# Branch A of an encoder layer: one round of transposes per step in place of two, with the scores behind it

## The chip, the core and the metric

The kernel runs on one core of a Trainium2 chip. The core has five engines with a queue each, and each queue runs its instructions in the order in which they were written. PE (TensorE) multiplies matrices and transposes tiles by multiplying with an identity; its results go to the eight banks of PSUM. DVE (VectorE) and ACT (ScalarE) read PSUM and SBUF, POOL (GpSimd) works on SBUF and issues some of the transfers, and SP (SyncE) issues the rest. An engine that needs another's result waits for a semaphore, and all that stands behind the waiting instruction waits too. The metric is the device time of one execution in microseconds, the median of several.

## The reference

An encoder layer is applied to a sample of 1024 positions and a prompt of 256, model width 1024. The part that matters here is branch A, an attention with 8 query heads of width 64 that share 2 key and value heads, a window of 128 positions to each side, a bias table and a sink per head:

```python
s = jnp.einsum('bnqgrd,bnkgd->bngrqk', qb, kb).astype(jnp.float32) * (dh ** -0.5)
...
logits = jnp.where(valid[None, :, None, None], s + bias, NEG_INF)
m = jnp.max(logits, axis=-1)
...
p = jnp.exp(logits - m[..., None])
denom = jnp.sum(p, axis=-1)
...
o = jnp.einsum('bngrqk,bnkgd->bnqgrd', p.astype(vb.dtype), vb).astype(jnp.float32)
```

A second branch (B, dilated windows) runs earlier in the kernel. Both are merged by gates, go through an output product and a squared-ReLU MLP, and a final norm. Everything is float32; the large products are split into high and low parts and multiplied in three passes.

## The kernel before, in words

Branch A covers 40 tiles: 4 units (two heads each) by 10 tiles of 128 queries (8 of the sample, 2 of the prompt). A tile sees W = 256 or 384 keys: three blocks of 128 inside the sample, two at its ends and for the prompt's tiles. The order of instructions is written out by hand. The main loop takes tiles two at a time, j = 0, 2, ... 40; I call one pass of it a step. In it stand:

- `scores(u, t)`: four products on PE into two banks of the tag `sc` (one per head), a DVE instruction per head that adds the bias, writes the logits `s` to SBUF and keeps the maximum, and a small DVE instruction, a SCALAR_TENSOR_TENSOR on line 1137, that makes the negated maximum `nm_a` of both heads.
- `exponential(u, t, h)`: ACT turns `s` into exp(s - maximum) in place, once per head.
- `transposes(u, t)`: PE transposes the 4 or 6 blocks of `s` into banks of the tag `pt`, four blocks to a bank; ACT moves the first bank to SBUF, DVE the second (lines 272 and 274).
- `values_of(u, t)`: PE multiplies values by the transposed weights of two tiles into the one bank of tag `pv`; DVE copies it out and POOL sends it to DRAM.
- `next(fill)`: one portion of an unrelated product, the plain gate logits (line 192): four matmuls of 512 columns or eight of 256. It fills PE's queue between the pieces of attention. At the end of a 512- or 256-column block ACT copies the bank out (`gs`), and after each 256-column block the next weights are split into `whi` (ACT) and `wlo` (DVE, line 235).
- `next(merges)`: one piece of the merging of branch B, work of POOL, DVE, ACT and the DMA queues (lines 1248 to 1272 on DVE, 1310 and 1313 on POOL).

PSUM has three banks of tag `mm` for the fill, two `sc`, two `pt`, one `pv`. Scores of step j are turned round by `transposes` in step j + 2 and used by `values_of` in step j + 4. Before the change a step in the middle is, on PE: scores, portion, values, portion, transposes of one tile, scores, portion, transposes of the other tile.

Of the kernel before, what the change touches and what calls it, by code (L numbers as in the profile page):

```python
# [15 lines left out]
P = 128  # L16
# [34 lines left out]
HALVES = (slice(0, HD), slice(HD, P))  # L51
# [46 lines left out]
def encoder_kernel(  # L98
# [5 lines left out]
    nc = tc.nc  # L104
# [31 lines left out]
    def bank(tag, name=None):  # L136
        return psum.tile([P, 512], F32, name=name or tag, tag=tag, bufs={"mm": 3, "sc": 2, "pt": 2, "pv": 1}[tag])
# [108 lines left out]
    ident = const.tile([P, P], F32, name="ident")  # L246
# [22 lines left out]
    def moved(eng, out, in_):  # L269

        if eng is nc.scalar:
            nc.scalar.activation(out, in_, AF.Copy)  # L272
        else:
            nc.vector.tensor_copy(out, in_)
# [48 lines left out]
    def steps_of(gen, n):  # L323
        for _ in range(n):
            next(gen, None)
# [152 lines left out]
    def attention_b(make):  # L478
# [21 lines left out]
        def load(j):  # L500

            if j >= n:
                return
            g, i, t, (pieces, W, _) = order[j]
            qk = held[j] = [make("qk", (P, 3 * P), n=4), None]
            for src, at, m, o in ((scr_qb[g][i], [x[2] for x in pieces], pieces[0][1], 0),
                                  (scr_kb[g][i], [x[3] for x in pieces], W, P)):
                if len(pieces) == 1:
# [8 lines left out]
        def load_v(j):  # L517
            if not 0 <= j < n:
                return
            g, i, t, (pieces, W, _) = order[j]  # L520
            v = held[j][1] = make("v", (P, 2, P), n=6)
            for a, (_, _, _, ka) in enumerate(pieces):
                for k in range(W // P):
                    nc.sync.dma_start(v[:, a + k, :], values_rows(g, i, ka // P + k))

        def scores(j):
# [4 lines left out]
            for k in (j, j + 1):  # L531
                g, i, t, (pieces, W, c0) = order[k]
                qk = held[k][0]
                for h in range(2):
                    rows = HALVES[h]
                    for a, (p0, nq, _, _) in enumerate(pieces):
                        nc.tensor.matmul(at(k, h)[p0 : p0 + nq, :], qk[rows, p0 : p0 + nq],  # L537
                                         qk[rows, P + P * a : P + P * a + W], start=True, stop=True,
                                         skip_group_check=True)
# [129 lines left out]
    with ExitStack() as pre:  # L669
# [195 lines left out]
        for t in range(2, NT):  # L865
# [13 lines left out]
            ps = bank("mm", "v")  # L879
# [20 lines left out]
        for t in (4, 5, 6, 7, 8, 9, 0, 1, 2, 3):  # L900
            ps = bank("mm", "v")
# [6 lines left out]
    if True:  # L908
# [177 lines left out]
        b, p = iter(()), parts0  # L1086
        att_b = iter(())
        for first, last, name in ((0, MIXED, "pairs"), (MIXED, len(PAIRS), "mixed")):
            with tc.tile_pool(name=name, bufs=1) as now[0]:
                if first:  # L1090
                    att_b = attention_b(stage)
                for j in range(first, last):
# [4 lines left out]
                    b, p = pair(b, p, PAIRS[j], PAIRS[j + 1] if j + 1 < len(PAIRS) else None, hooks, tick, first)  # L1097
# [10 lines left out]
    if True:  # L1108
# [4 lines left out]
        def a3(name, shape=(P, 2, 3 * P), n=3, dt=F32):  # L1113
            return att.tile(list(shape), dt, name=name, tag=name, bufs=n)

        tiles = []
# [4 lines left out]
        live, units = {}, {}  # L1121
# [19 lines left out]
        def exponential(u, t, h):  # L1141
            W, s = tiles[t][1], live[u, t]
            nc.scalar.activation(s[:, h, :W], s[:, h, :W], AF.Exp, bias=nm_a[:, 2 * u + h : 2 * u + h + 1, t],
                                 accum_out=l_a[:, 2 * u + h : 2 * u + h + 1, t])

        def transposes(u, t):

            W = tiles[t][1]
            s = live[u, t]
            pt = a3("pt", (P, 6, P), 2)  # L1150
            jobs = [(b, h) for b in range(W // P) for h in range(2)]
            for i, eng in ((0, nc.scalar), (4, nc.vector))[: 1 + (len(jobs) > 4)]:
                ps, e = bank("pt"), min(len(jobs), i + 4)
                for k, (b, h) in enumerate(jobs[i:e]):
                    nc.tensor.transpose(ps[:, P * k : P * k + P], s[:, h, P * b : P * b + P], ident)  # L1155
                moved(eng, pt[:, i:e, :], ps[:, : P * (e - i)].rearrange("p (i q) -> p i q", q=P))
            live[u, t] = pt

        def values_of(u, t):

            pv = bank("pv")
            for i in range(2):
                lo, W, _ = tiles[t + i]
                pt = live.pop((u, t + i))
                v, rest = units[u][0]["v"]
                for b in range(W // P):
                    k = lo + b
                    src = v[:, k, HALVES[u // 2]] if k < 8 else rest[:, k - 8, HALVES[u // 2]]
                    for h in range(2):
                        nc.tensor.matmul(pv[HALVES[h], P * i : P * i + P], src, pt[:, 2 * b + h, :],  # L1170
                                         start=b == 0, stop=b == W // P - 1, skip_group_check=True)
            o = a3("o", (P, 2, P), 2)
            nc.vector.tensor_copy(o, pv[:, : 2 * P].rearrange("p (i q) -> p i q", i=2))
            nc.gpsimd.dma_start(scr_o[t // 2][:, u], o)
# [156 lines left out]
    if True:  # L1331
# [53 lines left out]
        order = [(u, t) for u in range(4) for t in range(NT)]  # L1385
        n = len(order)
        fill = logits()
        merges = merge()
        next(merges)
        steps_of(fill, 2)  # L1390
        for j in range(0, n + 2, 2):
            if j < n:
                scores(*order[j])
                next(fill)
                for h in range(2):
                    exponential(*order[j], h)
            if j > 2:
                values_of(*order[j - 4])
                if j < n:
                    next(merges, None)  # L1400
            next(fill)
            if j:
                transposes(*order[j - 2])
            if j == n:
                next(fill)
            if j < n:
                scores(*order[j + 1])
                next(fill)
            if j:
                transposes(*order[j - 1])  # L1410
                if j > 2:
                    next(merges, None)
            if j < n:
                for h in range(2):
                    exponential(*order[j + 1], h)
            if j == n - 4:
                high_b(0)
                low_b(0)
            if j < n and order[j][1] == 0 and order[j][0] < 3:
                u = order[j][0] + 1  # L1420
                units[u] = load_unit(u), load_bias(u, lambda name, shape: a3(name, shape, 2))
            if j in (n - 6, n - 4):
                fetch()
            if j == n - 2:
                load_o(0)
                load_o(1)
# [9 lines left out]
        jobs = [(x, b, c) for b in range(3) for x in "ba" for c in range(KC if x == "b" else 4)]  # L1436
# [41 lines left out]
        for i, (x, b, c) in enumerate(jobs):  # L1478
            t0, n = BLOCKS[b]
# [13 lines left out]
            per, src = (4, (ob_hi, ob_lo)) if x == "b" else (2, (o_hi, o_lo))  # L1493
            cols = slice(P * (c % per), P * (c % per) + P)
            ps = bank("mm")
# [79 lines left out]
    with ExitStack() as pre:  # L1575
# [20 lines left out]
        for hh in range(2):  # L1596
# [17 lines left out]
            for t in range(NT):  # L1614
                m = parts.pop(t)
                ps = bank("mm")
# [43 lines left out]
    class Down:  # L1660
# [4 lines left out]
        def make(self, name, shape=(P, 2, 512), dt=F32):  # L1665
            return self.late.tile(list(shape), dt, name=name, tag="l4", bufs=8)
# [196 lines left out]
    with ExitStack() as pre:  # L1863
# [106 lines left out]
        b = b0, p0  # L1970
        down = Down()
        last = FF // P // 2 - 1
        for j in range(last + 1):
            b = up(j, *b, entering() if not j else down.begin() if j == last else iter(()))
# [26 lines left out]
```

## Time and profile before

| | us |
|---|---|
| median of 3 runs (1690.64 to 1692.21) | 1692.16 |
| the profiled execution | 1693.05 |
| its span, first to last instruction | 1691.3 |
| branch A's loop, from 543.7 to 679.7 of the span | 136.0 |

On the whole span PE is busy 1670.7 us (99%), DVE 950.1, ACT 721.3 and POOL 514.9. A busy share close to one means that little idle time is left to remove; it does not say that the matrix engine works at its peak. The timeline's rows give start, duration, engine, line, operation, output and inputs, shape and count, and in brackets the idle time before the row and what ended it. Matmuls overlap, so what one costs is read from the distance between starts: 0.23 us for 512 columns, 0.12 for 256, about 0.11 for a transposed block, while their durations are 0.39, 0.28 and 0.27.

### The profile page before, as it was taken

Reading aid. Unit: us, or ns where it says so; the run is one execution under the profiler, and the core shown is the slowest. Engines: PE = TensorE matmul, PEld = TensorE weight load, DVE = VectorE, ACT = ScalarE, POOL = GpSimd, SP = SyncE. Lnnn points to the kernel's source line nnn. Section 1 sums busy time; section 2 is a strip of 40 time slices with the busy share of each in tenths; the row PEclk is TensorE's granted clock in tenths of the full one; section 3 lists DMA queues with packets and bytes.
Section 4 is the critical chain, followed back from the end, with each engine's and each line's share of the span. In section 5 each row is a group of like instructions: output and inputs, shape, how many; then the busy total and the mean of one; then the engine's idle time right before and its main releaser. Section 6 shows DMA issues by size and latency. Waiting matters only on the chain.

```text
span 1691.3 us, 24932 instructions
## 1 busy us (share of the span) xinstructions
PE 1670.7 (99%) x9268; PEld 1414.9 (84%) x9268; DVE 950.1 (56%) x1548; ACT 721.3 (43%) x1489; POOL 514.9 (30%) x404
## 2 busy tenths in 40 slices
PE   8999999999999999999999999999999999999998
PEld 7898888887788888888888888888887888888886
DVE  6733233455563565667378445455457767667575
ACT  6332323356562656654176333333334333333345
POOL 1312212212112472200100556455556322314150
PEclk9999999999999999999999999999999999999999
DMA  7416562567666893845121443343346744633333
GB/s 246 151 57 125 134 136 75 162 192 200 182 196 193 219 245 100 289 136 189 41 85 58 159 159 118 121 159 130 116 152 250 280 152 157 209 106 116 119 119 124
DMA packets 224408, 260.35 MB, mean 154 GB/s; under 512 B 29568, under 2 KB 154288, under 8 KB 224288
## 3 DMA queue, kind: packets, MB, share of 16 engines
q1 hardware_dynamic: 214976, 235.60, 43.9%
q0 software_dynamic: 7936, 20.54, 5.6%
q10 hardware_dynamic: 1376, 2.62, 0.4%
q8 instruction: 73, 1.20, 0.3%
q14 instruction: 47, 0.39, 0.1%
HBM read 173.03 MB, written 90.92 MB: 156 GB/s over the span
## 4 chain that ended last, share of the span: by engine, by line
PE 90%; DVE 4%; ACT 2%; DMA 2%; issue 1%; POOL 1%; SPq 0%; DVEq 0%; ACTq 0%; POOLq 0%
PE dn L347 20%; PE x L347 18%; PE mm L192 14%; PE z L347 9%; PE v L794 6%; PE mm L347 5%; PE y L347 5%; PE sc L347 2%; PE pv L347 2%; PE sc L537 1%; PE pv L1170 1%; PE pv L582 1%; PE pt L569 1%; PE pt L1155 1%; PE sc L1131 1%
## 5 line engine op out<-in xcount | busy, mean ns | idle before, releaser
L347 PE MATMUL dn<-dhi,ulo 128*128 128x512 f32 x448 | 175.7, 392 | 4.3 <-DVE ulo L186 4.3
L347 PE MATMUL dn<-dlo,uhi 128*128 128x512 f32 x448 | 175.2, 391 | 0.0
L347 PE MATMUL dn<-dhi,uhi 128*128 128x512 f32 x448 | 175.1, 391 | 0.0
L347 PE MATMUL x<-chi,wlo 128*128 128x512 f32 x424 | 167.3, 395 | 1.7 <-DVE wlo L314 1.6
L347 PE MATMUL x<-clo,whi 128*128 128x512 f32 x424 | 165.7, 391 | 0.1
L347 PE MATMUL x<-chi,whi 128*128 128x512 f32 x424 | 165.1, 389 | 0.0
L314 DVE TENSOR_TENSOR wlo<-ta,whi 128x1024 fp32r<-128x1024 f32 x30 | 55.7, 1857 | 179.1 <-ACT whi L312 179.1
L314 DVE TENSOR_TENSOR wlo<-raw,whi 128x1024 fp32r<-128x1024 f32 x60 | 92.5, 1541 | 96.7 <-ACT whi L312 96.7
L389 POOL TENSOR_TENSOR tb<-raw 128x512 f32<-128x512 f32 x25 | 32.7, 1308 | 364.4 <-DMA raw<-in_w_in_dram 147.8
L347 PEld LDWEIGHTS dn<-dhi,ulo 128*128 128x128 f32 x448 | 84.6, 189 | 23.2 <-DVE ulo L186 5.7
L186 DVE TENSOR_TENSOR ulo<-uraw,uhi 128x1024 fp32r<-128x1024 f32 x56 | 94.3, 1702 | 12.4 <-ACT uhi L185 12.4
L347 PEld LDWEIGHTS dn<-dhi,uhi 128*128 128x128 f32 x448 | 84.7, 189 | 17.8
L347 PEld LDWEIGHTS dn<-dlo,uhi 128*128 128x128 f32 x448 | 84.7, 189 | 17.4
L347 PEld LDWEIGHTS x<-chi,wlo 128*128 128x128 f32 x424 | 79.8, 188 | 18.1 <-DVE wlo L314 1.3
L347 PEld LDWEIGHTS x<-chi,whi 128*128 128x128 f32 x424 | 79.6, 188 | 17.0
L1699 POOL TENSOR_TENSOR t<-raw,t 128x1024 f32<-128x1024 f32 x16 | 47.7, 3001 | 147.0 <-DMA raw<-in_w_down_dram 147.0
L347 PEld LDWEIGHTS x<-clo,whi 128*128 128x128 f32 x424 | 79.8, 188 | 14.8 <-DVE clo L314 0.4
L1853 DVE TENSOR_TENSOR v<-v,dn 128x512 f32<-128x512 f32 x90 | 59.6, 681 | 40.4 <-PE dn L347 37.9
L1946 POOL TENSOR_TENSOR u<-u,u 128x640 f32<-128x640 f32 x16 | 26.1, 1630 | 160.0 <-ACT u L1871 160.0
L347 PE MATMUL dn<-dhi,up 128*128 128x512 f32 x224 | 73.5, 389 | 0.0
L347 PE MATMUL z<-chi,wlo 128*128 128x512 f32 x184 | 72.0, 391 | 0.0
L272 ACT ACTIVATE pt<-pt 128x512 f32<-128x512 f32 (+1 forms) x70 | 37.9, 543 | 79.5 <-PE pt L1155 45.0
(325 smaller groups left out, 4660.9 us busy)
## 6 DMA issues: line engine op xcount, KB each, us to landing
scr_u<-u SPq DMA_DIRECT2D x112, 320.0 KB, 2.6
uraw<-scr_u SPq DMA_DIRECT2D x56, 512.0 KB, 4.5
raw<-in_w_in_dram SPq DMA_DIRECT2D x33, 512.0 KB, 5.4
raw<-in_w_up_dram SPq DMA_DIRECT2D x32, 512.0 KB, 5.2
raw<-in_w_down_dram SPq DMA_DIRECT2D x28, 512.0 KB, 6.6
sg<-scr_g SPq DMA_DIRECT2D x32, 256.0 KB, 6.4
uraw<-scr_u SPq DMA_DIRECT2D x28, 256.0 KB, 4.7
v<-scr_v SPq DMA_DIRECT2D x96, 64.0 KB, 2.7
```

What stands on the lines that cost most here:

```text
L186: nc.vector.tensor_tensor(lo, src, hi.bitcast(F32), op=ALU.subtract)
L192: nc.tensor.matmul(ps, a, b, start=i == 0, stop=i == len(seq) - 1)
L272: nc.scalar.activation(out, in_, AF.Copy)
L314: nc.vector.tensor_tensor(lo, src, hi.bitcast(F32), op=ALU.subtract)
L347: nc.tensor.matmul(ps, a, b, start=first and i == 0, stop=last and i == len(seq) - 1, skip_group_check=True)
L389: (nc.vector if vector else nc.gpsimd).tensor_tensor(o, x, y, op=ALU.subtract)
L537: nc.tensor.matmul(at(k, h)[p0 : p0 + nq, :], qk[rows, p0 : p0 + nq], qk[rows, P + P * a : P + P * a + W], start=True, stop=True, skip_gro ...
L569: nc.tensor.transpose(ps[:, P * a : P * a + P], s[:, h, P * k : P * k + P], ident)
L794: nc.tensor.matmul(ps[:, :n], a, b, start=k == 0 and j == 0, stop=k == KC - 1 and j == 2)
L1699: nc.gpsimd.tensor_tensor(o, a, b, op=ALU.subtract)
L1853: nc.vector.tensor_tensor(v, v, ps, op=ALU.add)
L1946: nc.gpsimd.tensor_tensor(u[S1], u21, u22, op=ALU.add)
```

## The change

In a step the values now come first, then the transposes of both tiles of the pair in one round, then the scores of the first tile, one portion of fill, the scores of the second tile, two portions. The round of transposes takes up to twelve blocks and three banks: the two `pt` banks and, where a pair has more than eight blocks, one of the three `mm` banks that the fill uses. ACT moves the first and third bank, DVE the second. The transposed weights of both tiles lie in one SBUF buffer of twelve blocks in place of two buffers of six. Portions of fill and pieces of the merge keep their number per step.

```diff
         def transposes(u, t):
 
-            W = tiles[t][1]
-            s = live[u, t]
-            pt = a3("pt", (P, 6, P), 2)
-            jobs = [(b, h) for b in range(W // P) for h in range(2)]
-            for i, eng in ((0, nc.scalar), (4, nc.vector))[: 1 + (len(jobs) > 4)]:
-                ps, e = bank("pt"), min(len(jobs), i + 4)
-                for k, (b, h) in enumerate(jobs[i:e]):
-                    nc.tensor.transpose(ps[:, P * k : P * k + P], s[:, h, P * b : P * b + P], ident)
-                moved(eng, pt[:, i:e, :], ps[:, : P * (e - i)].rearrange("p (i q) -> p i q", q=P))
-            live[u, t] = pt
+            pt = a3("pt", (P, 12, P), 1)
+            jobs, at = [], []
+            for i in range(2):
+                at.append(len(jobs))
+                jobs += [(live[u, t + i], b, h) for b in range(tiles[t + i][1] // P) for h in range(2)]
+            for i, tag, eng in ((0, "pt", nc.scalar), (4, "pt", nc.vector), (8, "mm", nc.scalar)):
+                if i < len(jobs):
+                    ps, e = bank(tag, "pt"), min(len(jobs), i + 4)
+                    for k, (s, b, h) in enumerate(jobs[i:e]):
+                        nc.tensor.transpose(ps[:, P * k : P * k + P], s[:, h, P * b : P * b + P], ident)
+                    moved(eng, pt[:, i:e, :], ps[:, : P * (e - i)].rearrange("p (i q) -> p i q", q=P))
+            for i in range(2):
+                live[u, t + i] = pt, at[i]
...
         for j in range(0, n + 2, 2):
+            if j > 2:
+                values_of(*order[j - 4])
+                if j < n:
+                    next(merges, None)
+            if j:
+                transposes(*order[j - 2])
             if j < n:
                 scores(*order[j])
                 next(fill)
                 for h in range(2):
                     exponential(*order[j], h)
-            if j > 2:
-                values_of(*order[j - 4])
-                if j < n:
-                    next(merges, None)
-            next(fill)
-            if j:
-                transposes(*order[j - 2])
-            if j == n:
-                next(fill)
-            if j < n:
                 scores(*order[j + 1])
-                next(fill)
-            if j:
-                transposes(*order[j - 1])
+                steps_of(fill, 2)
                 if j > 2:
                     next(merges, None)
-            if j < n:
                 for h in range(2):
                     exponential(*order[j + 1], h)
+            else:
+                steps_of(fill, 2)
+                next(merges, None)
```

On PE, in the first unit around the values of tiles 2 and 3 (`pv`: values, `mm`: fill, `pt`: transposes, `sc`: scores), the queue held before:

```order
L1170 MATMUL pv<-pt,va 64x128 x12
L192 MATMUL mm<-hhi,wlo 128x512
L192 MATMUL mm<-hlo,whi 128x512
L192 MATMUL mm<-hhi,whi 128x512
L192 MATMUL mm<-hhi,wlo 128x512
L1155 MATMUL pt<-ident,s 128x128 x6
L1131 MATMUL sc<-kk,q 128x256
```

and at the same values it now holds:

```order
L1173 MATMUL pv<-pt,va 64x128 x12
L1157 MATMUL pt<-ident,s 128x128 x12
L1131 MATMUL sc<-kk,q 128x384
L1132 MATMUL sc<-kk,q 128x384
L1131 MATMUL sc<-kk,q 128x384
L1132 MATMUL sc<-kk,q 128x384
L192 MATMUL mm<-hhi,whi 128x512
```

What follows the values is now a round of transposes where a portion of fill stood, and one round of twelve where there were two of six with scores and a portion between them.

On DVE, in the step j = 10, where a piece of the merge of branch B stands behind the copy of the values (`cb` is the merge's scratch tile, ISA on line 1133 adds the bias and keeps the maximum), the queue held before:

```order
L1137 SCALAR_TENSOR_TENSOR nm_a<-m,nsink 128x2
L1173 COPY o<-pv 128x256
L1259 TENSOR_TENSOR cb<-cb 128x120
L1260 TENSOR_TENSOR cb<-cb 128x40
L1261 TENSOR_TENSOR cb<-cb 128x40
L1263 RECIPROCAL cb<-cb 128x40
L1270 TENSOR_TENSOR cb<-cb 128x40
L1272 TENSOR_TENSOR cb<-cb 128x8x4
L1272 TENSOR_TENSOR cb<-cb 128x4x2
L1272 TENSOR_TENSOR cb<-cb 128x4x8
L1272 TENSOR_TENSOR cb<-cb 128x4x2
L1133 ISA s,m<-sc,bias 128x384
```

and now:

```order
L1176 COPY o<-pv 128x256
L1262 TENSOR_TENSOR cb<-cb 128x120
L1263 TENSOR_TENSOR cb<-cb 128x40
L1264 TENSOR_TENSOR cb<-cb 128x40
L1266 RECIPROCAL cb<-cb 128x40
L1273 TENSOR_TENSOR cb<-cb 128x40
L1275 TENSOR_TENSOR cb<-cb 128x8x4
L1275 TENSOR_TENSOR cb<-cb 128x4x2
L1275 TENSOR_TENSOR cb<-cb 128x4x8
L1275 TENSOR_TENSOR cb<-cb 128x4x2
L274 COPY pt<-pt 128x512
L1133 ISA s,m<-sc,bias 128x256
```

The logits behind the merge's piece were those of the step's second tile and are now those of its first, and a copy of a whole bank of transposes has come between.

More of the change, by code (lines that the diff above doesn't have):

```diff
@@ L1163, in values_of @@
                 lo, W, _ = tiles[t + i]
-                pt = live.pop((u, t + i))
+                pt, at = live.pop((u, t + i))
                 v, rest = units[u][0]["v"]
@@ L1169, in values_of @@
                     for h in range(2):
-                        nc.tensor.matmul(pv[HALVES[h], P * i : P * i + P], src, pt[:, 2 * b + h, :],
+                        nc.tensor.matmul(pv[HALVES[h], P * i : P * i + P], src, pt[:, at + 2 * b + h, :],
                                          start=b == 0, stop=b == W // P - 1, skip_group_check=True)
```

## The prediction

> **What bounds the kernel now.** I read the page first, its busy shares and the chain that ended last; then the window of branch A's loop; then who kept PE's weight loads waiting there; then the timeline of single steps.
>
> ```profile
> PE 1670.7 (99%) x9268; PEld 1414.9 (84%) x9268; DVE 950.1 (56%) x1548; ACT 721.3 (43%) x1489; POOL 514.9 (30%) x404
> ...
> PE 90%; DVE 4%; ACT 2%; DMA 2%; issue 1%; POOL 1%; SPq 0%; DVEq 0%; ACTq 0%; POOLq 0%
> ```
> ```profile
> 543.70:679.70 136.00, 135.45 (x1081) 115.96 (x1079) 73.57 (x264) 80.54 (x219) 67.49 (x82) 1.00 0.70 193
> ```
>
> PE carries the chain. In the 136.0 us of the loop it is busy for 135.45 at full granted clock, DVE and ACT for a little over half. So a new order can win only where PE's matmuls stand further apart than they need, and it loses wherever PE comes to wait.
>
> ```profile
> PEld pv L1170 <- issue: 4.1, 12, 0.4
> PEld mm L192 <- issue: 3.4, 20, 0.2
> PEld pv L1170 <- ACT s L1143: 1.1, 3, 0.4
> ...
> PEld sc L1131 <- DVE m L1133: 0.5, 2, 0.3
> ```
>
> Before the fill's weights, 20 times 0.17 us pass with nothing waited for: it is the first portion behind each group of values. Before the values themselves stands a similar gap. Nothing else on PE waits for long.
>
> **The change part by part.** First the order of values, fill and transposes. The timeline of PE behind a group of values in branch A:
>
> ```profile
> 594.92 1.53 PE L1170 MATMUL pv<-pt,va 128*64 128x128 f32 x24
> 596.38 0.50 PE L192 MATMUL mm<-hhi,wlo 128*128 128x512 f32 x1
> 596.72 0.40 PE L192 MATMUL mm<-hlo,whi 128*128 128x512 f32 x1
> 596.95 0.39 PE L192 MATMUL mm<-hhi,whi 128*128 128x512 f32 x1
> ...
> 597.41 0.82 PE L1155 MATMUL pt<-ident,s 128*128 128x128 f32 x6
> 597.98 0.36 PE L1131 MATMUL sc<-kk,q 128*128 128x256 f32 x1
> ```
>
> The first fill matmul keeps PE 0.34 us (596.38 to 596.72) where the next takes 0.23: 0.11 lost, beside the 0.17 ahead of it. The change puts transposes behind the values. Branch B has that pair of neighbours already:
>
> ```profile
> 423.74 1.09 PE L582 MATMUL pv<-pt,v 128*64 128x128 f32 x16
> 424.77 1.09 PE L569 MATMUL pt<-ident,s 128*128 128x128 f32 x8
> 425.61 0.36 PE L347 MATMUL mm<-phi,wlo 128*128 128x256 f32 x1
> ```
> ```profile
> PEld pt L569 <- issue: 3.9, 23, 0.2
> ```
>
> The wait ahead of the weights is 3.9 / 23 = 0.17 there too. The eight transposes take 0.84 us to the next start; six in branch A, not behind values, take 0.57 (597.41 to 597.98), so eight would take 0.57 + 2 x 0.11 = 0.79, and the loss is some 0.05 to 0.07 in place of 0.11. Each of the 19 steps that have values gains about 0.04 us: **-0.8 us**. From both sides: 0 (the two waits are equal) and -3.4 (the row of 20 waits gone altogether). I take the value from the same neighbours in branch B.
>
> [...]
>
> Second, the end of the loop, where before values stood right behind the transposes that feed other values:
>
> ```profile
> 673.28 0.60 PE L1155 MATMUL pt<-ident,s 128*128 128x128 f32 x4
> ...
> 674.17 1.31 PE L1170 MATMUL pv<-pt,va 128*64 128x128 f32 x20 [0.29 <-ACT pt L272]
> ...
> 679.16 0.66 PE L1170 MATMUL pv<-pt,vp 128*64 128x128 f32 x8 [0.16 <-ACT pt L272]
> ```
>
> Both idle times, 0.29 + 0.16, were waits for ACT's copies of transposes. Now two portions lie between the last transposes and their values, 8 x 0.23 = 1.9 us: **-0.5 us**, at least 0 and at most -0.7 with the starts around them.
>
> Third, whether PE finds its operands ready in a step. The latencies are those of one tile's scores:
>
> ```profile
> 579.61 0.42 PE L1131 MATMUL sc<-kk,q 128*128 128x384 f32 x1
> 579.87 0.34 PE L1132 MATMUL sc<-kk,q 128*128 128x384 f32 x1
> ...
> 580.39 0.39 PE L192 MATMUL mm<-hhi,whi 128*128 128x512 f32 x1
> ```
> ```profile
> 580.36 0.56 DVE L1133 CUSTOM_DVE_ANT_0 s<-sc,bias 128x384 f32<-128x384 f32 x1 [0.83 <-PE sc L1132]
> ...
> 581.43 0.16 DVE L1137 SCALAR_TENSOR_TENSOR nm_a<-m,nsink 128x2 f32<-128x2 f32 x1
> ```
> ```profile
> 581.69 0.61 ACT L1143 ACTIVATE s<-s,nm_a 128x384 f32<-128x384 f32 x1
> ...
> 582.90 0.58 ACT L1195 ACTIVATE gs<-mm 128x512 f32<-128x512 f32 x1
> ```
>
> Scores take PE 0.78 (579.61 to 580.39; 0.70 when no transposes stand ahead); DVE starts 0.49 behind the second matmul, the negated maximum starts 1.07 later, ACT 0.26 after that, and two exponentials take 1.21. With time 0 at the first value of a step whose tiles all have 384 keys: values to 1.46; twelve transposes to 2.75; scores j to 3.53; portion to 4.46; scores j+1 to 5.16; two portions to 7.03; next values 7.11; next transposes of tile j at 8.57 and of tile j+1, six blocks later, at 9.28. DVE: logits j start at 3.50, negated maximum 4.57; ACT: exponentials j 4.83 to 6.04, then `gs` where one is due, to 6.6. Logits j+1 start at 5.13, negated maximum to 6.36, exponentials 6.6 to 7.8. The need is at 9.28: 1.4 us to spare, about 0.4 where the split of weights (1.04 us of ACT) stands ahead of the exponentials, four times in the loop. The scores' banks: head 0 of tile j is read by 4.06 and wanted at 4.46, head 1 by 4.5 and wanted at 4.8. That is 0.3 to spare, against more than a microsecond before, when values and transposes lay between the two scores. DVE's copy of the second bank ends just ahead of the logits: eighth transpose at 2.28, copy from about 2.65 for 0.69, the longest of this row.
>
> ```profile
> L274 DVE COPY pt<-pt x54: 414/423/687, 359.5 to 672.2; 128x256 f32<-128x256 f32 x42, 128x512 f32<-128x512 f32 x12
> ```
>
> So an ordinary step costs nothing. In the first step with transposes (j = 2) no values stand ahead of them, which takes 1.46 from the spare time: **+0.2 us** (0 to 0.4).
>
> Fourth, DVE's piece of the merge, which now stands ahead of the logits whose bank the next scores want:
>
> ```profile
> 574.90 1.31 PE L1170 MATMUL pv<-pt,va 128*64 128x128 f32 x20
> ```
> ```profile
> 570.34 0.49 DVE L1248 COPY cb<-cb 128x64 f32<-128x64 f32 x4
> ...
> 571.21 0.28 DVE L1255 TENSOR_TENSOR cb<-cb 128x120 f32<-128x120 f32 x1
> ...
> 576.26 0.42 DVE L1173 COPY o<-pv 128x256 f32<-128x256 f32 x1 [1.35 <-PE pv L1170]
> 576.61 0.27 DVE L1259 TENSOR_TENSOR cb<-cb 128x120 f32<-128x120 f32 x1
> ...
> 578.29 0.55 DVE L1133 CUSTOM_DVE_ANT_0 s<-sc,bias 128x384 f32<-128x384 f32 x1
> ```
>
> In step j = 10 the piece takes 1.68 us (576.61 to 578.29). By the new order: values copied from 1.36 to 1.71, piece to 3.39, bank of transposes to 4.0, logits of head 0 (256 keys) to 4.4. PE: values to 1.25, eight transposes to 2.09, scores to 2.65, portion to 3.58, and there the next scores want that bank: 0.9 us lost. In step j = 8 the piece takes 1.15 (570.34 to 571.49) behind longer values, and the same count gives 0.3. Together **+1.2 us** (0 to 2.8, the length of both pieces).
>
> Fifth, POOL. From 591 to 648, some nine steps of 6.7 us (136.0 over 20 steps and a bit), POOL multiplies and adds rows of branch B, and the negated maximum, 0.16 us otherwise, stretches to POOL's end:
>
> ```profile
> 606.18 1.31 DVE L1137 SCALAR_TENSOR_TENSOR nm_a<-m,nsink 128x2 f32<-128x2 f32 x1
> ```
> ```profile
> 591.15 2.02 POOL L1310 TENSOR_TENSOR merged<-r 128x512 f32<-128x512 f32 x1 [0.53 <-PE pt L1155]
> ...
> 605.91 1.56 POOL L1313 TENSOR_TENSOR merged<-merged,r 128x512 f32<-128x512 f32 x1
> ...
> 647.11 0.81 POOL L1313 TENSOR_TENSOR merged<-merged,r 128x256 f32<-128x256 f32 x1
> ```
> ```profile
> L1137 DVE SCALAR_TENSOR_TENSOR nm_a<-m,nsink 128x2 f32<-128x2 f32 x40 | 12.2, 306 | 1.4
> ```
> ```profile
> 624.80 1.23 DVE L235 TENSOR_TENSOR wlo<-raw,whi 128x1024 fp32r<-128x1024 f32 x1 [1.83 <-DMA r<-scr_c]
> ```
>
> Both end at 607.5. Over the 40 instructions the stretching is 12.2 - 40 x 0.16 = 5.8 us. Each step has two of them in a row ahead of the exponentials; 1.4 us to spare covers all but a rare double. A split of weights that waits, as at 624.80 (1.83 us), now stands ahead of the next step's copies and logits rather than behind the logits. For both I take **+1.0 us**: one long double and one late split of about 0.5 each; 0 if the spare time covers all, some 7 if it covers none (next part).
>
> [...]
>
> The rest moves nothing: ACT's copies per pair stay two, DVE's become one of 512 columns for two of 256; the third bank comes from the fill's three, and each portion's first bank was emptied at least a step earlier. SP and POOL keep their order of transfers. The sum is -0.8 - 0.5 + 0.2 + 1.2 + 1.0 = **+1.1 us**: 1694.1 against the profiled execution's 1693.05, which is 0.9 above the median of the runs; against the median of 1692.16, **1693.3**. A difference below 0.2% (3.4 us) can hardly be told from none.
>
> **The rivals.** *Late exponentials in the merging steps (slower).* POOL's train starts behind the copy of the values, now at a step's start, so its adds of 1.56 us lie over both negated maxima of a step. If both are held by 1.4 us, the second ends at 8.5, the exponentials at 9.9, and PE waits 0.6 to 0.7 at the second tile's transposes. It decides from 1.4 us of delay per step. Nine such steps give 6.3 beside the 0.1 of the other terms without the fifth: 1698.6. For it speaks the phase; against it, that the longest pair before (1.31 and 0.52) adds only 1.5, and the pairs around it less than 1.0. *The gap behind the values vanishes (faster).* With -3.4 for the first term, -0.5 at the end and no new wait, 1688.3. Branch B's 3.9 us row speaks against it. *Nothing comes of it:* two gaps a step stay as large, the waits are covered, 1692.2.
>
> **How the numbers follow.** My sum: 0.62, its own range 1691.0 to 1695.5 (terms two and four at their ends). Late exponentials: 0.25, from 1695 up to 1701. Nothing: 0.06. The gap vanishes: 0.07. The range 1690.0 to 1698.0 leaves out the upper half of the second and all of the last, and about 0.2 in all. Faster by over 0.2%: 0.07; within: 0.68; slower: 0.25.
>
> **What would show it.** Right: waits before the weights of `pt` on PE by issue, some 19 times 0.17, where `mm` had them; a wait of about 1 us of the scores for DVE's maxima near 576 and a shorter one near 570; none of the last values for ACT's copies; branch A's loop 136 to 138 us long. Wrong: repeated waits of PE's transposes for ACT's exponentials between 590 and 650 (the first rival); no wait by issue behind the values (the second); or a loss outside the loop, for which I have no term.

## The result and the profile after

The changed kernel takes **1686.59 us** (median of 7 runs, 1685.27 to 1688.7) against 1692.16 (7 runs, 1690.56 to 1695.35): a ratio of **0.9967, interval 0.9957 to 0.9976**. That is 5.6 us faster, where the prediction said 1693.3 and gave faster 7 in 100. The profiled execution took 1685.92 us, with a span of 1684.1.

The page after, its busy shares, the chain, and the costliest group, that of the first product of the MLP's down phase; then that last row of the page before:

```profile
PE 1667.8 (99%) x9268; PEld 1413.9 (84%) x9268; DVE 952.2 (57%) x1544; ACT 718.3 (43%) x1485; POOL 511.6 (30%) x404
...
PE 92%; DVE 3%; ACT 2%; DMA 1%; issue 1%; SPq 1%; POOL 0%; DVEq 0%; ACTq 0%
...
L347 PE MATMUL dn<-dhi,ulo 128*128 128x512 f32 x448 | 174.5, 390 | 2.0 <-DVE ulo L186 2.0
```
```profile
L347 PE MATMUL dn<-dhi,ulo 128*128 128x512 f32 x448 | 175.7, 392 | 4.3 <-DVE ulo L186 4.3
```

Branch A's loop after, as one stretch (columns: its bounds, its length, busy time of PE, PEld, DVE, ACT and POOL, granted clock, DMA share, GB/s), and PE's waits in it (total us, times, longest):

```profile
542.05:677.56 135.51, 134.46 (x1081) 116.00 (x1079) 79.16 (x261) 78.25 (x215) 66.45 (x82) 1.00 0.69 192
```
```profile
PEld pv L1173 <- ACT s L1143: 2.8, 8, 0.4
PEld pt L1157 <- issue: 2.6, 15, 0.2
PEld pv L1173 <- issue: 2.1, 6, 0.4
PEld sc L1131 <- DVE m L1133: 1.9, 4, 1.2
PEld pt L1157 <- ACT s L1143: 1.4, 6, 0.5
...
PE sc L1131 <- DVE m L1133: 0.7, 1, 0.7
```

The loop looks much as forecast, with gaps of 0.17 us ahead of the transposes and a wait for VectorE's maxima. It is only half a microsecond shorter. The rest of the 5.6 us is not in it. Measured on TensorE, from its first scores to its last values, the loop takes 135.81 and 136.47 us in two profiles of the kernel before, 135.50 and 135.12 in two of the changed one. From the first transposes behind the loop (`pt<-ident,wl`) to the twentieth `dn` matmul of the down phase, which I call **the entry** from here on, the two kernels take 617.2 and 618.5 against 612.1 and 612.4. In between they run in step, but for a few tenths, until about 1280. After the entry both need 384 us to the end. (The two profiled executions are 7.2 us apart in span; 1.7 us of that lie ahead of the loop, where this execution of the kernel before waits 1.8 us for `qk` near 459.)

So the gain is made some 600 us behind the code that was changed. TensorE there, first before, then after (start, length, the idle time ahead in brackets):

```profile
1299.56 0.80 PE L347 MATMUL dn<-dhi,ulo 128*128 128x512 f32 x1 [3.19 <-DVE ulo L186]
1300.15 0.63 PE L347 MATMUL dn<-dlo,uhi 128*128 128x512 f32 x1
1300.58 0.63 PE L347 MATMUL dn<-dhi,uhi 128*128 128x512 f32 x1
```
```profile
1294.07 0.40 PE L347 MATMUL dn<-dhi,ulo 128*128 128x512 f32 x1
1294.31 0.40 PE L347 MATMUL dn<-dlo,uhi 128*128 128x512 f32 x1
...
1296.85 0.50 PE L347 MATMUL dn<-dhi,ulo 128*128 128x512 f32 x1 [1.23 <-DVE ulo L186]
```

Before, TensorE waits 3.19 us for `ulo`, the low half of the first left operand, and then its matmuls start 0.43 us apart (1300.15 to 1300.58) instead of 0.24. The stretches show why, again before and after (the granted clock stands third from the end):

```profile
1299.50:1303.00 3.50, 3.06 (x7) 1.96 (x7) 3.50 (x3) 1.22 (x3) 3.50 (x2) 0.50 0.04 14
```
```profile
1297.00:1300.00 3.00, 3.00 (x14) 2.46 (x15) 3.00 (x2) 0.93 (x1) 3.00 (x2) 1.00 0.11 40
```

The trace's clock record has it at one half from 1298.41, in the middle of the wait, to 1305.24, and full from the first 5 us on till the last 4 otherwise. The sum fits: idle time 3.19 + 0.38 (a second wait at 1302.87) against 1.23 makes 2.3 us, and half of the 5.7 us from 1299.56 to 1305.24 makes 2.8, together 5.1, which is the difference between the entries of the two profiles (617.2 - 612.1).

What makes `ulo` late? Backwards along the chain: VectorE's two `ulo` and GpSimd's two `t`, first before, then after:

```profile
1296.14 6.68 DVE L186 TENSOR_TENSOR ulo<-uraw,uhi 128x1024 fp32r<-128x1024 f32 x2
```
```profile
1296.05 5.68 POOL L1699 TENSOR_TENSOR t<-raw 128x1024 f32<-128x1024 f32 x2 [3.98 <-DMA raw<-in_w_down_dram]
```
```profile
1292.24 4.56 DVE L186 TENSOR_TENSOR ulo<-uraw,uhi 128x1024 fp32r<-128x1024 f32 x2
```
```profile
1292.64 6.40 POOL L1698 TENSOR_TENSOR t<-raw 128x1024 f32<-128x1024 f32 x2 [4.46 <-DMA raw<-in_w_down_dram]
```

Before, GpSimd starts 0.09 us ahead of VectorE and each `ulo` takes 3.4 us. After, VectorE is 0.4 ahead, its first `ulo` takes 1.2 and only the second is stretched. VectorE is later because ScalarE is, and ScalarE is later because it issues the first four loads of the down phase's weights (`raw`), one of which has to wait (ACTq is ScalarE's sequencer):

```profile
1274.71 7.21 ACTq L1673 DMA_DIRECT2D raw<-in_w_down_dram  x3
1281.96 1.06 ACT L312 ACTIVATE whi<-tb 128x1024 fp32r<-128x1024 f32 x1 [6.28 <-DMA scr_u<-u]
```
```profile
1272.74 5.17 ACTq L1672 DMA_DIRECT2D raw<-in_w_down_dram  x3
1277.96 1.06 ACT L312 ACTIVATE whi<-tb 128x1024 fp32r<-128x1024 f32 x1 [4.24 <-POOL u L1948]
```

Three issues take 7.21 us before and 5.17 after. The last of them waits on the landing of an earlier store, `scr_u<-u`, which took 6.87 us before and 4.83 after (the row after names GpSimd's `u` instead, which ended within 0.4 us of that landing). Two microseconds are lost in the DMA queues, then. What is different in them? The DMA view of the 8 us from the first of the four issues, before; the microsecond ahead of that issue, after; and the 8 us from it, after (queue: packets, MB, share of 16 engines; then the loads with their size and median us to landing):

```profile
q1 hardware_dynamic: 484, 1.12, 40.3%
q8 instruction: 1, 0.02, 0.8%
...
raw<-in_w_down_dram ACTq DMA_DIRECT2D x4, 512.0 KB, 8.0
```
```profile
q8 instruction: 1, 0.02, 6.6%
```
```profile
q1 hardware_dynamic: 498, 1.15, 41.2%
...
raw<-in_w_down_dram ACTq DMA_DIRECT2D x4, 512.0 KB, 6.7
```

A packet of 16 KB, of the kind "instruction", stands before in the middle of the four loads (1278.66, 4.5 us behind the first issue) and after just ahead of them (1271.59, 0.6 us ahead). The page counts 73 such packets on this queue in either kernel. There is one for every 127 matmuls on the mean (9,268 to 73), each with its weight load, so I take them for TensorE's own code, though the trace names no engine for them. And TensorE's instructions have moved against the work. The trace has 15,481 instructions of TensorE (weight loads, matmuls, waits) ahead of the first `dn` in the kernel before, 15,499 in the changed one. All 18 more are wait instructions, 321 instead of 303.

### The profile page after: what moved, and what is told of

It reads as the page before. It is cut to its first block, busy times and chain, and to the rows that moved or that the text cites. A ratio compares the mean times of both kernels' runs of the same rounds, so it can differ in the third digit from the quotient of the medians.

```text
span 1684.1 us, 24915 instructions
## 1 busy us (share of the span) xinstructions
PE 1667.8 (99%) x9268; PEld 1413.9 (84%) x9268; DVE 952.2 (57%) x1544; ACT 718.3 (43%) x1485; POOL 511.6 (30%) x404
## 4 chain that ended last, share of the span: by engine, by line
PE 92%; DVE 3%; ACT 2%; DMA 1%; issue 1%; SPq 1%; POOL 0%; DVEq 0%; ACTq 0%
PE dn L347 20%; PE x L347 19%; PE mm L192 14%; PE z L347 9%; PE v L794 5%; PE mm L347 5%; PE y L347 5%; PE sc L347 3%; PE pv L347 3%; PE pv L1173 1%; PE pt L1157 1%; PE sc L537 1%; PE pv L582 1%; PE pt L569 1%; PE sc L1131 1%
## 5 line engine op out<-in xcount | busy, mean ns | idle before, releaser
L186 DVE TENSOR_TENSOR ulo<-uraw,uhi 128x1024 fp32r<-128x1024 f32 x56 | 92.4, 1669 | 11.6 <-ACT uhi L185 11.6
L347 PEld LDWEIGHTS x<-clo,whi 128*128 128x128 f32 x424 | 79.8, 188 | 14.8 <-DVE clo L314 0.4
L347 PE MATMUL z<-chi,whi 128*128 128x512 f32 x184 | 71.6, 389 | 0.0
```

What stands on the lines that cost most here:

```text
L186: nc.vector.tensor_tensor(lo, src, hi.bitcast(F32), op=ALU.subtract)
L347: nc.tensor.matmul(ps, a, b, start=first and i == 0, stop=last and i == len(seq) - 1, skip_group_check=True)
```

## The experiments

My theory from here is **code reload**: the extra instructions shift the point at which TensorE's code is fetched, and the packet no longer meets the loads at the entry. Its rivals: **buffers**, since the new loop may leave other tile buffers to all that follows; **the loop itself**; and chance.

**Both kernels again**, unchanged.

> The kernel before once more, unchanged, for a second profile. Both theories: branch A's loop (first scores to last values) again 135.8 us. Theory 'chance' (the 5 us outside the loop are waits for transfers that fall differently in each execution): the wait of 1.8 us for qk near 459 and the wait of 3.2 us for ulo near 1300 do not both come back. Theory 'phase' (the loop's new timing sets them): both come back, within 0.3 us each.

> The changed kernel once more, unchanged, for a second profile. Both theories: ratio to before 0.9967 as measured, loop 135.5 us. Chance: a wait near 459 or 1300 shows up in it, or the profile's span differs by over 2 us from 1684.1 while the loop stays. Phase: span 1684 to 1685, no wait near 459, about 1.2 us for ulo near 1295.

The kernel before gave 1691.89 us (ratio 1.0, 0.9989 to 1.0011), the changed one 1686.11 (0.9967, 0.9954 to 0.9979), and each had its own entry again (618.5 and 612.4): the wait for `ulo` is 3.3 us in the one and 1.4 in the other. That rules chance out for the entry. The wait for `qk` near 459 did not come back, so those 1.8 us were chance.

**One round per tile, in the new order.** The order of the changed kernel, but `transposes` and `values_of` as in the kernel before: each tile's transposes in a round of their own through the two `pt` banks.

```diff
             if j:
                 transposes(*order[j - 2])
+                transposes(*order[j - 1])
```

> The new order of a step, but each tile's transposes in a round of their own through the two pt banks (no third bank, two buffers of six). The second tile's first bank must wait for ACT's copy of the first tile's: 0.8 us in pairs of twelve, 0.5 in pairs of ten, none in pairs of eight, so 2.9 us a unit and 11.6 us over the loop: 1698 against 1686.6. If instead DVE's and ACT's queues hide it, under 3 us.

1696.69 us, ratio 1.003 (1.0018 to 1.0042). Its loop as one stretch, and PE's longest waits in it:

```profile
543.04:687.92 144.88, 137.07 (x1081) 115.94 (x1079) 75.94 (x265) 82.00 (x219) 67.48 (x82) 1.00 0.66 179
```
```profile
PEld pt L1155 <- ACT pt L272: 11.4, 16, 0.9
...
PE pt L1155 <- ACT pt L272: 6.2, 13, 0.5
```

The second round waits for ScalarE's copy out of the first one's bank, and the loop is 9.0 us longer than 135.9, and 9.6 longer than the changed kernel's, where I had expected 11.6. The order alone loses without the third bank. The total is only 4.8 us worse than the 1691.94 of the kernel before on the same chip, because its entry, 612.5 us, is that of the changed kernel: it has 19 more instructions on TensorE.

**First scores ahead of the values.** The joint round through three banks, but the first tile's scores, portion and exponentials stay at the head of the step as in the kernel before.

```diff
         for j in range(0, n + 2, 2):
+            if j < n:
+                scores(*order[j])
+                next(fill)
+                for h in range(2):
+                    exponential(*order[j], h)
             if j > 2:
                 values_of(*order[j - 4])
...
             if j < n:
-                scores(*order[j])
-                next(fill)
-                for h in range(2):
-                    exponential(*order[j], h)
                 scores(*order[j + 1])
```

> The joint round of transposes through three banks, but the first tile's scores and their portion stand ahead of the values as before. If the pieces of the merge ahead of the logits cost the 1.9 us that PE waited for DVE in the changed kernel's loop, the loop is 1.5 to 2 us shorter than 135.5; if those waits only take the place of others, it is the same within 0.5.

1688.65 us, ratio 0.9981 (0.9971 to 0.999). The loop is the shortest of all, and TensorE has no idle time in it:

```profile
543.03:676.40 133.37, 133.37 (x1081) 116.36 (x1079) 79.79 (x261) 78.37 (x215) 67.72 (x82) 1.00 0.72 196
```

That is two microseconds shorter than the changed kernel's loop, a little more than I had expected, and yet the whole is 2 us slower: the entry is at 615.9, with two instructions fewer than before and the packet 4.8 us behind the first load.

**Twenty TensorE instructions, and nothing else.** At the start of the kernel, where TensorE waits for its first operands, `warm` issues dummy matmuls that nobody reads (four instructions each). Five more of them push all later code back by 20 instructions and leave every buffer, order and wait behind them as it was.

```diff
-        warm(15)
+        warm(20)
```

> The kernel before with 20 instead of 15 dummy matmuls in its first 8 us, where TensorE waits for the first transposes anyway (in the trace of before it is idle from 6.6 to 7.9); the loop, the order and every buffer stay as before, only 20 more TensorE instructions stand ahead of everything that follows (the changed kernel has 18 more ahead of the down phase). Theory code fetch: the 16 KB packet that reloads TensorE's instructions, which in before and its copy falls 4.5 and 4.2 us behind the first load of the down phase's blocks (1278.66 against 1274.15; 1279.39 against 1275.14) and in the changed kernel and its copy 0.6 us ahead of it and 0.1 us behind it, moves to the changed kernel's place; the wait of the first dn matmuls for ulo shrinks from 4.3 to about 2.0 us, the stretch from the first transposes behind the loop to the twentieth dn matmul from 617 or 618 to about 612 us, and the time is 1686 to 1688, with the old loop. Theory buffers (the loop's order decides which buffer each later tile gets): nothing changes, 1691 to 1693. Theory gain of the loop itself: 1691 to 1693 too.

**1687.99 us, ratio 0.997 (0.9959 to 0.9982)**, with the loop of before (136.04 us). ScalarE's sequencer in it, and TensorE at the entry:

```profile
1274.68 5.62 ACTq L1673 DMA_DIRECT2D raw<-in_w_down_dram  x3
```
```profile
1298.75 0.50 PE L347 MATMUL dn<-dhi,ulo 128*128 128x512 f32 x1 [1.19 <-DVE ulo L186]
```

The packet went to 0.8 us ahead of the first load, the landing of the fourth load from 14.7 to 12.8 us behind it, and the entry to 612.4. Five dummy matmuls give most of what the change gives. Buffers and loop are out as main causes.

The reverse, on the changed kernel:

```diff
-        warm(15)
+        warm(10)
```

> The changed kernel with 10 instead of 15 dummy matmuls at its start, so 20 TensorE instructions fewer ahead of the down phase and the rest untouched. Theory code fetch: the packet falls some 4.5 us behind the first load again, the wait for ulo is back at 2.8 to 4.4 us, and the time is 1689.5 to 1691.5, with the new loop. Theory buffers: 1686 to 1687.5 as the changed kernel. Theory gain of the loop itself: the same 1686 to 1687.5.

1693.05 us, ratio 0.9999 (0.999 to 1.0008): with the new loop (135.26 us) and 20 instructions fewer, the gain is gone. The packet is 4.6 us behind the first load, the entry at 617.0, with a wait of 2.8 us and the clock at one half behind it. The time is 1.6 us above what I expected. In its profile the stretch ahead of the loop is 2 to 4 us longer than in the changed kernel's; part of that is this edit's own, since with ten dummy matmuls the full clock came at 13.6 us instead of 5 to 6 (TensorE is busy for 10.73 us of the first 14 with 49 matmuls, against 10.32 with 62) and the first product behind them at 13.7 instead of 12.1; the rest I cannot place.

**The dose.** The kernel before with 20 fewer, 40 more and 60 more (`warm` of 10, 4, 2; of 20, 9, 2; of 20, 9, 7 instead of 15, 4, 2).

> The kernel before with 5 dummy matmuls (20 TensorE instructions) fewer at its start; nothing else changes. It moves the code packet later, to some 7 us behind the first load of the down phase's blocks (before: 4.5). Theory code fetch, with the cost where the packet meets the first loads in flight (the first four loads and the seven stores of u take from 0 to some 15 us behind the first issue): the entry stays slow, 614 to 618 us from the first transposes behind the loop to the twentieth dn matmul, time 1689 to 1694. If instead any shift of the code helps (the old place being bad for another reason), the entry is near 612 and the time near 1687.

> The kernel before with 10 dummy matmuls (40 TensorE instructions) more at its start, 5 in each of two stretches where TensorE waits. The code packet falls some 3 us ahead of the first load of the down phase's blocks and the next one some 23 us behind it. Theory code fetch: the entry is as in the changed kernel, 612 to 613 us, and the time 1686.5 to 1688.5, as with 20 more. If 20 more instructions helped by chance of timing, the entry goes back to 616 to 618 and the time to 1691 to 1693.

> The kernel before with 15 dummy matmuls (60 TensorE instructions) more at its start. The packet falls some 5.5 us ahead of the first load and the next one some 20 us behind it, where the second loads are in flight. Theory code fetch: the first loads stay quick; the second packet meets loads of which some are not wanted at once, so the entry is 612 to 615 us and the time 1687 to 1690.

They gave 1689.2 (ratio 0.9984, 0.9974 to 0.9993), 1687.24 (0.9967, 0.9955 to 0.998) and 1687.69 us (0.9975, 0.9966 to 0.9984).

**The shortest loop with a good entry.** The order with the first scores ahead of the values, with 20 and with 40 more.

> The joint round with the first tile's scores, portion and exponentials ahead of the values (the experiment that gave 1688.65 and whose loop took 133.36 us, the shortest), with 20 instead of 15 dummy matmuls at the start. Theory code fetch: the entry of the down phase as in the changed kernel, so 1688.65 less 3 to 4 us, 1684 to 1686, which is faster than both kernels. Theory buffers: 1688 to 1689, unchanged.

> The joint round with the first tile's scores ahead of the values (loop of 133.4 us), with 40 more TensorE instructions at the start; 20 more left its entry at 614.9 us, with VectorE's ulo still late by 2.1 us. Theory code fetch alone: with the packet 3 us ahead of the first load the entry is 612 to 614 us and the time 1684 to 1686. If the rest of that entry's delay comes from elsewhere (GpSimd's subtractions, which waited for TensorE's z there, by another buffer), it stays at 614 to 615 and the time at 1686 to 1687.

With 20 more, 1686.37 us (0.9963, 0.995 to 0.9975), 0.4 us above the range that I gave; with 40 more **1684.82 us (0.9955, 0.9942 to 0.9967)**, the lowest median of all. With 20 more the packet is away, but GpSimd's `t` began 0.05 us ahead of VectorE's first `ulo`, and the entry stayed at 614.9. With 40 more VectorE was first, by 0.5 us, and it is 612.7. What tips that race here, with the same landing of the fourth load, I did not settle.

All kernels side by side, from their traces (the ratios above are to runs of the kernel before on the same chip, whose medians were 1691.94, 1692.63 and 1692.23 us). "Instructions" are TensorE's ahead of the first `dn`, against the kernel before; "packet" is the start of the 16 KB packet, and "fourth landing" the landing of the fourth load, both from the issue of the first load; "lead" is how far VectorE's first `ulo` starts ahead of GpSimd's `t` beside it (below zero: behind); all but instructions and the last column (median) from one profile each, in us.

| kernel | instructions | packet | fourth landing | lead | entry | loop | time |
|---|---|---|---|---|---|---|---|
| before | 0 | +4.5 | 14.7 | -0.09 | 617.2 | 135.81 | 1692.16 |
| before, again | 0 | +4.2 | 14.8 | -0.06 | 618.5 | 136.47 | 1691.89 |
| first scores ahead | -2 | +4.8 | 14.0 | -0.26 | 615.9 | 133.36 | 1688.65 |
| changed, 20 fewer | -2 | +4.6 | 14.0 | -0.15 | 617.0 | 135.26 | 1693.05 |
| before, 20 fewer | -20 | +6.9 | 14.5 | +0.05 | 615.4 | 135.88 | 1689.2 |
| changed | +18 | -0.6 | 12.8 | +0.40 | 612.1 | 135.50 | 1686.59 |
| changed, again | +18 | +0.1 | 13.1 | +0.46 | 612.4 | 135.12 | 1686.11 |
| one round per tile | +19 | 0.0 | 12.9 | +0.53 | 612.5 | 144.88 | 1696.69 |
| before, 20 more | +20 | -0.8 | 12.8 | +0.70 | 612.4 | 136.04 | 1687.99 |
| first scores ahead, 20 more | +18 | -0.4 | 12.9 | -0.05 | 614.9 | 133.35 | 1686.37 |
| before, 40 more | +40 | -2.5 | 12.7 | +0.80 | 612.3 | 135.11 | 1687.24 |
| first scores ahead, 40 more | +38 | -2.4 | 12.9 | +0.50 | 612.7 | 133.37 | 1684.82 |
| before, 60 more | +60 | -3.8 | 13.1 | +0.04 | 612.5 | 135.82 | 1687.69 |
| changed, merge last (below) | +18 | -0.6 | 14.5 | +0.09 | 613.7 | 134.87 | 1686.23 |

With 20 instructions fewer, none, 20, 40 and 60 more in the kernel before, the packet goes from +6.9 over +4.5, -0.8 and -2.5 to -3.8: its place follows TensorE's instructions, as I would expect of TensorE's code. A packet between 4 and 7 us behind the first load goes with a fourth landing at 14.0 to 14.8 us, in all five rows that have one; a packet up to 4 us ahead of it, or with it, goes with 12.7 to 13.1, in eight rows of nine. The ninth is the last row: two packets of 8 KB, of the same kind from another queue, fall among the loads (1.1 and 4.6 us behind the first), and the fourth landing is late again. That the loads land up to 2 us later where a packet of about 1 us meets them is measured; how it delays them the trace doesn't tell.

The entry needs one thing more, the race of `ulo` and `t`. Of the six rows with a late landing four have GpSimd first, of the eight with an early one a single one. With an early landing and VectorE first, the entry is 612.1 to 612.7. With a late landing alone, it is 613.7 and 615.4; the latter holds 1.4 us that arise near 703, where TensorE waits 1.17 us for `wlo`. A lost race alone gives 614.9. Both together give 615.9 to 618.5 (the 618.5 holds 1.2 us from near 703 too), and in three of these four the clock falls as well. So, by one profile each, a late landing alone costs about 1.5 us; the rest of the 5 comes when the race is lost too, and a few hundredths of a microsecond decide that.

**The merge's pieces at the end of the step.** For the term of the prediction that was worth most in the loop.

```diff
                 values_of(*order[j - 4])
-                if j < n:
-                    next(merges, None)
...
-                if j > 2:
-                    next(merges, None)
                 for h in range(2):
                     exponential(*order[j + 1], h)
+                if j > 2:
+                    next(merges, None)
+                    next(merges, None)
```

> The changed kernel with both pieces of the merge at the end of each step, behind the second tile's exponentials, instead of one behind the values and one behind the portions; TensorE has the same number of instructions. If the pieces on VectorE ahead of the negated maxima cost what the waits for m show in the changed kernel (1.9 us over four times), the loop is 133 to 134 us instead of 135.1 to 135.5 and the time about 1684.7. If the pieces then stand in the way of the copies of the next step's transposes or values, the loop stays at 135 to 136 and the time at 1686 to 1688.

1686.23 us (0.996, 0.9946 to 0.9974), not to be told from the changed kernel. PE's waits for the maxima in its loop:

```profile
PEld sc L1131 <- DVE m L1133: 1.4, 3, 0.9
...
PE sc L1131 <- DVE m L1133: 0.5, 1, 0.5
```

The wait near 576, 1.16 us in the changed kernel, is 0.23 here; another, near 643, has grown from 0.23 to 0.93. The loop is 134.87 us: 0.4 of the 1.9 us came back. That lies just under the second range that I had given for the loop, and the time lies in the second range: the pieces in their new place hold up most of what they held up before.

## Why the prediction was wrong

**The step that failed** is the sentence "The rest moves nothing", which ends the count of the change's parts, and with it the sum that has, in the prediction's words, no term for "a loss outside the loop", nor for a gain. It followed the work, its order, its copies and its transfers. It did not count instructions. The change adds 18 wait instructions on TensorE, and they move the 16 KB packet that I take for TensorE's code reload from the middle of the first loads at the entry (4.5 us behind the first issue) to just ahead of them (0.6 us). That is worth about 5 us (617.2 against 612.1 in the first pair of profiles; 618.5, less the 1.2 from near 703, against 612.4 in the second), more than all five terms together. The kernel before with 20 instructions more and the old loop has it too.

The bound was read right as far as it went: TensorE carries the chain. But "a new order can win only where PE's matmuls stand further apart than they need" looked at the loop alone. TensorE's 3.19 us of idle time near 1300 and the half clock behind it were in the trace of before, outside the window that I read.

**The loop's terms.** Their sum was +1.1; the loop got 0.6 shorter (135.86 as the mean of six profiles with the old loop, 135.11 to 136.47; 135.29 of three with the new one). With the first scores ahead of the values the loop has the gains and no waits for maxima worth naming, and it is 2.5 us shorter than the old one. The distances between TensorE's starts tell where.

- *Transposes behind the values (-0.8).* Right in place and in size. Ahead of `pt` there are 15 waits by issue of 0.17, where the fill had 20. A portion behind values took 1.03 us against 0.93 elsewhere, so 0.10 is gained; a round of twelve with both tiles' scores takes 2.77 where two rounds of six with their scores took 2.71, so 0.06 is lost. The difference is the 0.04 a step that was counted.
- *The end of the loop (-0.5).* Right in place, half the size: it went by the idle times of 0.29 + 0.16. By the starts, two rounds of four transposes took 0.89 and 0.53 there instead of 0.36, and sixteen values 1.20 instead of 0.82, together 1.1 us, and all of it is gone.
- *A gain without a term.* The split of weights at 624.80, which the prediction put among the losses to come, was a loss already. TensorE's transposes behind it, in the kernel before:

```profile
625.75 1.10 PE L1155 MATMUL pt<-ident,s 128*128 128x128 f32 x6
```

  The next start, at 626.89, is 1.14 us away instead of 0.57, and the scores there take 0.94 instead of 0.78: 0.7 us, and 0.9 to 1.2 in two other profiles of the old loop. The changed kernel has no wait there. The shortest old loop, 135.11, has none either. The three gains make 2.6.
- *First step (+0.2).* No wait of TensorE above 0.2 us shows there.
- *The merge's pieces on VectorE (+1.2: 0.9 in j = 10, 0.3 in j = 8).* Right in place and in size (by the starts 0.9 and 0.2):

```profile
573.73 0.27 DVE L1262 TENSOR_TENSOR cb<-cb 128x120 f32<-128x120 f32 x1
...
575.42 0.68 DVE L274 COPY pt<-pt 128x512 f32<-128x512 f32 x1
576.02 0.41 DVE L1133 CUSTOM_DVE_ANT_0 s<-sc,bias 128x256 f32<-128x256 f32 x1
```
```profile
576.49 0.45 PE L1131 MATMUL sc<-kk,q 128*128 128x384 f32 x1 [0.74 <-DVE m L1133]
```

  The piece (from 573.73) and the copy stand ahead of the logits, as counted; TensorE waits 0.74 at 576.49, its weight load 1.16, and at 569.41 the weight load waits 0.32.
- *GpSimd's hold on the negated maximum (+1.0).* One wait of TensorE's transposes for exponentials, at 614.51, idle for 0.27 us. By the starts, ten transposes there take 1.81 us instead of 1.07, which is 0.7; in the other two profiles of this loop it is 0.3 and 0.5. No split of weights holds TensorE up. So the term was somewhat too large.

Gains of 2.5 us against 1.3, and losses of 1.9 (the loops 135.29 and 133.36 apart) against 2.4: two errors on the same side, 1.7 us in all.

**The rivals.** Late exponentials didn't come: between 590 and 650 TensorE's matmuls wait for ScalarE once, at 614.51. That the gap behind the values vanishes gave a number close to the result, 1688.3, for a reason that didn't happen: the gaps are still there, 2.6 us ahead of the transposes and 2.1 + 2.8 ahead of the values.

**The range** of 1690 to 1698 was built from the loop's terms and could not hold a term of 5 us elsewhere.

## What to carry to other kernels

Before crediting a reorder with a gain or a loss of a few microseconds, compare the stretches that it does not touch, and look there for the first lasting difference. Count TensorE's instructions, waits included, ahead of each place where loads are short of time: here 18 to 20 more moved an instruction packet from 4.5 us behind the first load to 0.6 or 0.8 us ahead of it, and 20 fewer moved it back to 4.6 behind. A few dummy instructions at a place where the engine is idle tell at once whether that is the cause. A variant should be judged by the loop's own length and the entry's apart; by total time the shortest loop here looked worse than a longer one, until forty instructions were added.

## What the runs showed of the hardware

- **Packets of instructions take part in DMA traffic.** 73 packets of 16 KB, of the kind "instruction", in a run of 1,690 us, one for 258 TensorE instructions on the mean (18,849 records of them in the trace of before; 18,849 / 73 = 258). That they are TensorE's code is my reading of this count and of the packet's shift from +6.9 to -3.8 us with 20 fewer to 60 more. A packet takes about 1 us (0.97 at the entry before, 1.06 after); where one falls 4 to 7 us behind the first of a burst of 512 KB loads, the fourth lands at 14.0 to 14.8 us instead of 12.7 to 13.1.
- **A wait of 3 us cost as much again.** In the kernel before, TensorE waited 3.19 us for `ulo`; its clock fell to one half 2.0 us into that wait (1298.41, idle from 1296.4) and stayed there for 6.83 us, until 1305.24, of which 2.8 us are lost by the sum above. In two more profiles with a slow entry, with waits of 3.3 us (before, again) and 2.8 (changed, 20 fewer), the first product stands at a clock of 0.50 too; the mean granted clock of these three is 0.997. In the eleven other profiles, with a mean of 0.999 or 1.0, it did not fall at the entry: in ten of them TensorE's longest wait for `ulo` was 1.0 to 2.1 us, but the eleventh (first scores ahead) waited 2.8 us and kept the full clock. What tells the two waits of 2.8 us apart was not shown.
- **Who comes first on VectorE and GpSimd decided here.** The same `ulo` takes 1.2 us when it starts ahead of GpSimd's `t`, be it by 0.04 us (60 more), and 3.4 when it starts 0.05 us behind it (first scores ahead, 20 more).
